# A decoder trunk on one core: biases loaded in nine pieces beside nine feed-forward tiles, and the residual's loads set between other loads

## The chip, the core and the metric

The kernel runs on one core of a Trainium2 chip. A core has five engines, each with its own queue of instructions that it works off in order: TensorE (PE in the rows; its weight loads are PEld), VectorE (DVE), ScalarE (ACT), GpSimd (POOL) and SyncE (SP), which here issues the transfers between DRAM and the on-chip memory (SBUF). The metric is the time of one execution on the device, in microseconds (us).

## The reference, cut to what matters

One step of a decoder trunk, for a prompt of 1024 tokens and 8 single new tokens, all float32, width 1024. Layer A is a gated linear recurrence, layer B an attention over a window of 128 tokens with 16 query heads on 4 shared key/value heads; each layer is followed by a SwiGLU feed-forward block, and every sub-layer is added to the residual:

```python
h = h + gate(c) * F(rmsnorm(h) * (1 + scale(c)) + shift(c))

def swiglu(x, w_in, w_out):                     # d_ff = 2816
    gate, up = jnp.split(x @ w_in, 2, axis=-1)
    return (jax.nn.silu(gate) * up) @ w_out

def rel_bias_for(dist, rel_bias):
    bias = rel_bias.astype(jnp.float32)[t5_bucket(dist)]
    ...
```

The attention adds that bias, one number for each head and distance, to its logits, and a learned sink for each head joins its softmax. The 8 new tokens attend to a cache of the last 128 rows of K and V, in which the new token's row takes the place of the oldest; the shifted caches are results too.

## The kernel before, in words

The tokens (1032 with the new ones) lie along the free axis, the features on the partitions, in 8 blocks of 128. A float32 product is three matmuls on rounded operands (`mm3`, L291 to L293): high by high, high by low, low by high. `weight()` (L178) makes the two halves of a weight tile: ScalarE casts it (L182), GpSimd subtracts the cast from it (L185). So a product needs, in this order, the weight's transfer, a cast on ScalarE and a subtraction on GpSimd.

The feed-forward block `ffn` (L1481) works through 22 tiles of 128 hidden columns. Tiles 2 to 21 go through `seven_products` (L1529): both halves of the SwiGLU input as one 2 by 2 block product with seven block products instead of eight (1, 2, 6, 7, 5, 3, 4 in the order used), each 24 matmuls of 128 x 258. The weights of these come from `seven` (L233): two raw tiles for a hidden tile, each in two transfers of 256 KB (L243), then three sums of them on VectorE (L253 to L255), a fourth later (L260), and seven units for the ring of 8 weight tiles. Units are prepared six ahead of their use. Of a tile's products, the first one's results are copied out by ScalarE (two COPYs, L1552), the others are added by VectorE (L1554 to L1571), with two Silu pairs on ScalarE (L1555, L1567), and the tile is stored to DRAM on SP (`ff`, L1572) as its last step.

`biases()` (L1296) prepares what layer B's attention needs beside the weights. It is called in the middle of the first feed-forward block, at tile 11: it loads a one-hot table, the bias table and a mask (L1302 to L1304), multiplies them in a small matmul with a sum (L1306, L1308), stores the result `rd` to DRAM, spreads it there to 128 rows (`gd`, 3 MB), loads the sinks (`sk`, `skd`) and the decode tokens' biases row by row for 8 tokens (L1319 to L1321), copies the two caches shifted by one row into the results (L1322, L1323), and negates the sinks (L1325).

The second place lies where layer B's attention ends and its output projection begins. `attention(1)` (second half of the heads) and `decode_attention()` run interleaved with the projection's products; the projection's results are added to the residual by VectorE (L845). The residual lies in DRAM (`hsc`) and is loaded in four chunks of 258 tokens by `reload_stack` (L1424, moves at L658, two transfers a chunk): the first chunk before, the others after `decode_attention` has issued the caches (L1769) and the new token's rows into them (`nd`, L1774).

The order of each engine's queue is fixed before the run by the Tile framework's scheduler, from its own estimates, and doesn't follow the order in which the code is written, except where `keep_in_program_order` (`fix` for a transfer) pins an instruction. A transfer on SP also waits for one of eight semaphores in turn, which the transfer eight issues earlier sets when it has landed.

Of the kernel before, what the change touches and what calls it, by code (L numbers as in the profile page):

```python
# [17 lines left out]
P = 128  # L18
# [8 lines left out]
NF = DFF // P  # L27
# [30 lines left out]
def bc(ap, axis, n):  # L58
    u = ap.unsqueeze(axis)
    shape = list(u.shape)  # L60
    shape[axis] = n
    return u.to_broadcast(shape)
# [3 lines left out]
def trunk_kernel(  # L66
# [40 lines left out]
    pe, act, dve, pool, sp = nc.tensor, nc.scalar, nc.vector, nc.gpsimd, nc.sync  # L107
# [10 lines left out]
    def nm(s):  # L118
        uid[0] += 1
        return f"{s}_{uid[0]}"  # L120

    def big(dt=F32, cols=TOK, parts=P):
        return p4.tile([parts, cols], dt, tag="c4", name=nm("c4"))
# [11 lines left out]
    def axp():  # L135
        return pp.tile([P, 512], F32, tag="ax", name=nm("ax"), bufs=4)
# [11 lines left out]
    class Stream:  # L148
# [15 lines left out]
        def next(self):  # L164
            n, room = self.used + 1, self.look
            while n < len(self.specs) and self.size[n] <= room:
                room -= self.size[n]
                n += 1
            self.ahead(n)
            u = self.done[self.used]  # L170
            self.used += 1
            return u
# [322 lines left out]
    fix = tc.keep_in_program_order  # L495
# [460 lines left out]
    X = Rows(KT)  # L956
# [339 lines left out]
    def biases():  # L1296

        stage = big(cols=1024)
        oneh = stage[:32, 0:384]
        relb = stage[:32, 384:400]  # L1300
        outs = stage[:16, 400:784]
        sp.dma_start(oneh, k_onehot)  # L1302
        sp.dma_start(relb, rel_bias)
        sp.dma_start(outs, k_outside)  # L1304
        ps = axp()
        pe.matmul(ps[:16, :384], relb, oneh, start=True, stop=True)  # L1306
        rrow = outs
        dve.scalar_tensor_tensor(rrow, ps[:16, :384], 8.0, outs, op0=ALU.mult, op1=ALU.add)  # L1308
        rd = dp.tile([16, 384], F32, name="rd")
        gd = dp.tile([16, P, 384], F32, name="gd")  # L1310
        sp.dma_start(rd, rrow)
        sp.dma_start(gd, bc(rd, 1, P))
        sk = cst.tile([P, 16], F32, name="sk")
        fix(sp.dma_start(sk, sinks_b[0].partition_broadcast(P)))
        skd = cst.tile([P, 1], F32, name="skd")
        late = cst.tile([P, 2 * P], F32, tag="early", name="late")
        biasd = late[:, 0:P]
        for b in range(NB):
            fix(sp.dma_start(skd[16 * b : 16 * b + 16, :], sinks_b[0].unsqueeze(1)))  # L1319
            sp.dma_start(biasd[16 * b : 16 * b + 16, 1:P], rd[:, P : 2 * P - 1])  # L1320
            sp.dma_start(biasd[16 * b : 16 * b + 16, 0:1], rd[:, 2 * P - 1 : 2 * P])  # L1321
        fix(sp.dma_start(ck_sample[:, 0 : WIN - 1], cache_swa_k[:, 1:WIN]))  # L1322
        fix(sp.dma_start(cv_sample[:, 0 : WIN - 1], cache_swa_v[:, 1:WIN]))  # L1323
        for t in (sk, skd):
            tc.keep_in_program_order(dve.tensor_scalar(t, t, -1.0, None, op0=ALU.mult))  # L1325
        return late, biasd, gd, sk, skd

    for hh in range(NH):
        first = hgrn_proj(hh) if hh else hgrn_first()
# [59 lines left out]
    def wo_second(o, gate, m, back, beside=iter(()), end=(3, 5)):  # L1389
        tdec = small([P, KT, NB], "tdec", 2)  # L1390
        us = [ws.next() for _ in range(4)]
        st = res[-1]
        N = StackNorm(st)
        x = Quads()

        def then(c):
            st.move(back, [c], False)
            yield from N.finish(c, *((3, 8) if c < G4.last else end))
            yield LAG
            yield from N.apply_steps(c, m, x)  # L1400

        for c in range(G4.n):
            for n in range(KT):
                wo_product(us[n // 2], o, c, n, gate, tdec, G4, anyp)
                N.square(c, n)
                step()
                if c and ((c - 1) * KT + n) % 2 == 0:
                    next(beside, None)
            if c == G4.last:
                residual_dec(tdec)  # L1410
                N.square_dec()
            queue(then(c))
        for _ in beside:
            pass
        return x, st
# [9 lines left out]
    def reload_stack(src, g):  # L1425

        st = Stack(g)
        res.append(st)
        st.move(src, [0], True)
        yield  # L1430
        st.move(src, range(1, g.n), True)


    def factors(x, st):
# [46 lines left out]
    def ffn(l, x, st, hs, norm, aside=None):  # L1481
# [115 lines left out]
                    pass  # L1597

        for j in range(PLAIN, NF):
            if j == NF // 2 and aside:  # L1600
                aside()
            seven_products(j, back if j == NF - 1 else None)

# [52 lines left out]
    back = [dp.tile([KT, P, T], F32, name=f"hs{i}") for i in range(2)]  # L1656
    X, st = wo_second(o, 16, 1, back[0], conditioning((6, 3), (2, 3)))
# [27 lines left out]
            yield from self.apply_steps(c, 2, self.x, keep=True)  # L1685

    bs = []
    nkv = ffn(0, X, st, back[0], ToKV, lambda: bs.extend(biases()))
    late, biasd, gd, nsk, nskd = bs


# [2 lines left out]
    X = Triples(KT)  # L1694
# [68 lines left out]
    def decode_attention():  # L1763
        kst, vst = [], []
        for dst, src in ((kst, cache_swa_k), (vst, cache_swa_v)):
            for hb in range(2):
                t = big(cols=T).rearrange("p (b f) -> p b f", b=4)
                bs = slice(4 * hb, 4 * hb + 4)
                sp.dma_start(t, src[bs].rearrange("b s h d -> s b (h d)"))  # L1769
                dst.append(t)  # L1770
        for dst, c0 in ((kst, 0), (vst, 256)):
            for hb in range(2):
                bs = slice(4 * hb, 4 * hb + 4)
                sp.dma_start(dst[hb][0:1], nd[bs, c0 : c0 + 256].unsqueeze(0))  # L1774
        ld = small([P, P], "s", 3)
        psl = axp()
        for hb in range(2):
            for a in range(2):
                ps = axp()
                for j in range(4):  # L1780
                    pe.transpose(
                        ps[:, j * P : (j + 1) * P], kst[hb][:, j, a * P : (a + 1) * P], ident
                    )
                kb = big(cols=512)
                act.copy(kb, ps)
                for j in range(4):
                    b = 4 * hb + j
                    c0 = 16 * b + 8 * a
                    pe.matmul(
                        psl[:, c0 : c0 + 8],  # L1790
                        kb[:, j * P : (j + 1) * P],
                        qdec[:, a, b].rearrange("p h g -> p (h g)"),
                        start=True,
                        stop=True,
                    )
                yield
        dve.tensor_copy(ld, psl[:, 0:P])
        ps = axp()
        pe.transpose(ps[:, 0:P], ld, ident)
        lt = small([P, P], "s", 3)  # L1800
        mx = small([P, 1], "dmx", 1)
        es = small([P, 1], "des", 1)
        den = small([P, 1], "dden", 1)
        dve.tensor_tensor_reduce(
            lt, ps[:, 0:P], biasd, -0.125, nskd, ALU.add, ALU.min, mx
        )
        act.activation(es, nskd, AF.Exp, scale=-1.0, bias=mx)
        act.activation(lt, lt, AF.Exp, scale=-1.0, bias=mx, accum_out=den)
        dve.tensor_tensor(den, den, es, op=ALU.add)
        dve.reciprocal(den, den)  # L1810
        dve.tensor_scalar(lt, lt, den, None, op0=ALU.mult)
        yield
        ps = axp()
        pe.transpose(ps[:, 0:P], lt, ident)
        dve.tensor_copy(ld, ps[:, 0:P])
        ps = axp()
        psv = ps[:, 0:64].rearrange("p (a b g) -> p a b g", a=2, b=NB)
        for b in range(NB):
            for a in range(2):
                for hf in range(2):  # L1820
                    kv = 2 * a + hf
                    pe.matmul(
                        psv[64 * hf : 64 * hf + 64, a, b, :],
                        vst[b // 4][:, b % 4, 64 * kv : 64 * kv + 64],
                        ld[:, 16 * b + 4 * kv : 16 * b + 4 * kv + 4],
                        start=True,
                        stop=True,
                    )
            if b % 2:
                yield  # L1830
        for a in range(2):
            dve.tensor_copy(adec[:, 4 * a : 4 * a + 4, :], psv[:, a].rearrange("p b g -> p g b"))
        yield
# [141 lines left out]
    loads = reload_stack(hsc, G4)  # L1975
    next(loads)
    next(second)
    dec = decode_attention()
    next(dec)
    for _ in loads:  # L1980
        pass

    def dec_first(o=o):
        for _ in dec:
            pass
        mixed_dec(o, adec, 0)
# [4 lines left out]
    X, st = wo_second(o, 64, 4, back[1], end=(5, 5))  # L1991
# [163 lines left out]
```

## Time and profile before

| | us |
|---|---|
| median of 3 runs | 2501.37 (2498.51 to 2503.21) |
| the profiled execution | 2500.0 |
| its span, first to last instruction | 2498.1 |
| TensorE busy in it | 2454.3 (98%) |
| VectorE busy | 1390.8 (56%) |
| ScalarE busy | 903.0 (36%) |
| GpSimd busy | 774.6 (31%) |

The mean granted clock of TensorE is 0.996 of the full one. A row of a timeline in the section below gives the start and the duration of an instruction or a run of like ones, the engine, its line in the kernel, what it writes and reads, the tile shapes and, in brackets, how long the engine had been idle before it and what it then waited for. Matmuls overlap in their pipeline, so the step from one start to the next is shorter than a matmul's duration. A name such as `wu` is a weight tile (high and low half), `raw` its unrounded tile, `mm` and `ax` two accumulation banks, `xq` the activations, `c` a buffer of general use and `hs` a chunk of the residual.

### The profile page before, as it was taken

The numbers are of one execution on the slowest core, as the hardware profiler recorded it, in microseconds if no ns is written. First come the engines' busy times: TensorE is split into PE (matmuls) and PEld (weight loads), VectorE is DVE, ScalarE is ACT, GpSimd is POOL, SyncE is SP. The second block draws the span as 40 slices with busy tenths as digits, with TensorE's granted clock in tenths as the row PEclk, the third lists the DMA queues.
The fourth block names the chain that finished last, engine by engine and source line by source line (L and its number), as shares of the span: only waits on it lengthen the run. The fifth ranks groups of instructions, "written<-read, shape, count | busy, mean of one in ns | idle before, by whom it ended". The sixth has DMA issues, their size and how long they took to land.

```text
span 2498.1 us, 52373 instructions
## 1 busy us (share of the span) xinstructions
PE 2454.3 (98%) x21557; PEld 2338.0 (94%) x21557; DVE 1390.8 (56%) x3177; ACT 903.0 (36%) x2012; POOL 774.6 (31%) x560
## 2 busy tenths in 40 slices
PE   7999999999999999999999999999999999999998
PEld 5999999998889999999999998878999999999998
DVE  6444444456486554656433735576885555565436
ACT  5333333332363332333211555454643333333112
POOL 1211111111225444544432131002364444445221
PEclk9999999999999999999999999999999999999999
DMA  9465522246833224326321322523222222264101
GB/s 332 146 214 178 170 76 72 70 131 211 267 106 94 82 84 144 97 83 233 123 77 51 93 56 65 165 85 110 69 86 77 77 77 81 82 228 148 65 26 69
DMA packets 314561, 293.43 MB, mean 117 GB/s; under 512 B 28681, under 2 KB 291738, under 8 KB 314290
## 3 DMA queue, kind: packets, MB, share of 16 engines
q1 hardware_dynamic: 313920, 289.86, 35.8%
q8 instruction: 170, 2.79, 0.5%
q14 instruction: 69, 0.57, 0.1%
q10 hardware_dynamic: 402, 0.22, 0.0%
HBM read 231.27 MB, written 63.99 MB: 118 GB/s over the span
## 4 chain that ended last, share of the span: by engine, by line
PE 89%; DVE 4%; DMA 3%; issue 2%; ACT 1%; SPq 0%; POOL 0%; ACTq 0%; DVEq 0%; POOLq 0%
PE mm L291 20%; PE mm L293 19%; PE mm L292 19%; PE ax L291 6%; PE ax L292 6%; PE ax L293 6%; PE ax L470 2%; PE ax L1943 1%; PE ax L1872 1%; PE ax L1098 1%; PE ax L1929 1%; PE ax L1225 1%; PE ax L1188 1%; DMA raw<-in_w_ffn_in_dram 1%; DMA gd<-rd 1%
## 5 line engine op out<-in xcount | busy, mean ns | idle before, releaser
L185 POOL TENSOR_TENSOR wu<-raw,wu 128x512 fp32r<-128x512 f32 x460 | 628.5, 1374 | 1380.1 <-ACT wu L182 1279.4
L291 PE MATMUL mm<-c,wu 128*128 128x344 f32 (+1 forms) x2104 | 673.8, 320 | 2.8 <-ACT c L917 1.7
L293 PE MATMUL mm<-c,wu 128*128 128x344 f32 (+1 forms) x2104 | 660.6, 314 | 1.9 <-issue 1.9
L292 PE MATMUL mm<-c,wu 128*128 128x344 f32 (+1 forms) x2104 | 662.0, 315 | 0.3 <-DVE c L920 0.3
L182 ACT CAST wu<-raw 128x512 fp32r<-128x512 f32 x464 | 286.0, 620 | 665.8 <-PE mm L293 358.5
L291 PEld LDWEIGHTS mm<-c,wu 128*128 128x128 f32 x2104 | 397.4, 189 | 16.1 <-issue 9.4
L292 PEld LDWEIGHTS mm<-c,wu 128*128 128x128 f32 x2104 | 397.8, 189 | 4.2 <-issue 2.6
L293 PEld LDWEIGHTS mm<-c,wu 128*128 128x128 f32 x2104 | 397.9, 189 | 1.8 <-issue 1.8
L291 PE MATMUL mm<-xq,wu 128*128 128x258 f32 x1376 | 390.3, 284 | 2.4 <-ACT wu L182 1.0
L293 PE MATMUL mm<-xq,wu 128*128 128x258 f32 x1376 | 389.6, 283 | 1.3 <-POOL wu L185 1.3
L292 PE MATMUL mm<-xq,wu 128*128 128x258 f32 x1376 | 388.2, 282 | 1.2 <-DVE xq L838 1.2
L291 PE MATMUL ax<-xq,wu 128*128 128x258 f32 x1120 | 316.4, 282 | 0.0
L293 PE MATMUL ax<-xq,wu 128*128 128x258 f32 x1120 | 315.8, 282 | 0.0
L292 PE MATMUL ax<-xq,wu 128*128 128x258 f32 x1120 | 315.6, 282 | 0.0
L291 PEld LDWEIGHTS mm<-xq,wu 128*128 128x128 f32 x1376 | 259.6, 189 | 4.1 <-DVE c L1502 1.2
L292 PEld LDWEIGHTS mm<-xq,wu 128*128 128x128 f32 x1376 | 260.7, 189 | 1.7 <-DVE xq L838 1.7
L293 PEld LDWEIGHTS mm<-xq,wu 128*128 128x128 f32 x1376 | 259.7, 189 | 2.8 <-POOL wu L185 1.5
L845 DVE SCALAR_TENSOR_TENSOR hs<-mm,ada,hs 128x344 f32<-128x344 f32 (+3 forms) x228 | 120.7, 533 | 173.3 <-PE mm L293 164.4
L292 PEld LDWEIGHTS ax<-xq,wu 128*128 128x128 f32 x1120 | 212.1, 189 | 0.0
L291 PEld LDWEIGHTS ax<-xq,wu 128*128 128x128 f32 x1120 | 211.5, 189 | 0.0
L293 PEld LDWEIGHTS ax<-xq,wu 128*128 128x128 f32 x1120 | 211.1, 188 | 0.0
L845 DVE SCALAR_TENSOR_TENSOR c<-mm,ada,c 128x344 f32<-128x344 f32 (+1 forms) x132 | 74.8, 571 | 112.1 <-PE mm L293 111.4
(329 smaller groups left out, 3603.1 us busy)
## 6 DMA issues: line engine op xcount, KB each, us to landing
c<-in_w_ada_dram SPq DMA_DIRECT2D x96, 512.0 KB
raw<-in_w_ffn_in_dram SPq DMA_DIRECT2D x160, 256.0 KB
ff<-c SPq DMA_DIRECT2D x44, 516.0 KB
c<-ff SPq DMA_DIRECT2D x44, 516.0 KB
raw<-in_w_ffn_out_dram SPq DMA_DIRECT2D x44, 512.0 KB
raw<-in_w_in_a_dram SPq DMA_DIRECT2D x32, 512.0 KB
hs<-hs SPq DMA_DIRECT2D x16, 516.0 KB
out_dram<-c SPq DMA_DIRECT2D x16, 512.0 KB
```

Of the source, the lines that this page charges most:

```text
L182: i = act.copy(u[:, 0, :], src)
L185: j = eng.tensor_tensor(u[:, 1, :], src, u[:, 0, :], op=ALU.subtract)
L291: put(pe.matmul(ps, wh, xh, start=first, stop=False))
L292: put(pe.matmul(ps, wh, xl, start=False, stop=False))
L293: put(pe.matmul(ps, wl, xh, start=False, stop=last))
L470: pe.matmul(ada_ps[q][32 * j : 32 * j + 32, 256 * i : 256 * i + 256], cT[:, k, :], u[i][:, j, :], start=(k == 0 and i == 0), stop=(k == KT ...
L845: dve.scalar_tensor_tensor(hc, ps[:, : g.pl[c]], ada[:, gate + n, 0:1], hc, op0=ALU.mult, op1=ALU.add)
L1098: pe.matmul(ps[32 * j : 32 * j + 32, c * 32 : (c + 1) * 32], KS[:, t0 : t0 + 32], QP[:, t0 : t0 + 32], start=True, stop=True, tile_positio ...
L1188: pe.matmul(ps[:, j * P : (j + 1) * P], kt[:, s], vt[:, s], start=True, stop=True)
L1225: pe.matmul(o, attT[:, c, :], vt[:, s], start=(c == 0), stop=True)
L1872: pe.matmul(psv[hf][:, gi, s0:256], q[2 * gp + gi][r, tb * P : (tb + 1) * P], kT[a][r, (tb - 1) * P + s0 : (tb + 1) * P], start=True, stop ...
L1929: pe.transpose(ps[:, g * P : (g + 1) * P], L[:, g, sb * P : (sb + 1) * P], ident)
```

## The change

`biases()` is a generator now. It is advanced once at each hidden tile from 11 on, before that tile's products, until it ends: nine pieces for tiles 11 to 19. Two more of its transfers are pinned to their place in the code. The residual's chunks are moved in three steps with a stop after each, and `decode_attention` stops between the caches and the new token's rows, so that its caller can put the loads in between: chunk 1 ahead of the caches, chunks 2 and 3 ahead of the rows. No operation on data is added or removed.

```diff
--- before.py
+++ after.py
@@ -1302,13 +1302,16 @@
         sp.dma_start(oneh, k_onehot)
         sp.dma_start(relb, rel_bias)
         sp.dma_start(outs, k_outside)
+        yield
         ps = axp()
         pe.matmul(ps[:16, :384], relb, oneh, start=True, stop=True)
         rrow = outs
         dve.scalar_tensor_tensor(rrow, ps[:16, :384], 8.0, outs, op0=ALU.mult, op1=ALU.add)
         rd = dp.tile([16, 384], F32, name="rd")
         gd = dp.tile([16, P, 384], F32, name="gd")
+        yield
         sp.dma_start(rd, rrow)
+        yield
         sp.dma_start(gd, bc(rd, 1, P))
         sk = cst.tile([P, 16], F32, name="sk")
         fix(sp.dma_start(sk, sinks_b[0].partition_broadcast(P)))
@@ -1317,13 +1320,16 @@
         biasd = late[:, 0:P]
         for b in range(NB):
             fix(sp.dma_start(skd[16 * b : 16 * b + 16, :], sinks_b[0].unsqueeze(1)))
-            sp.dma_start(biasd[16 * b : 16 * b + 16, 1:P], rd[:, P : 2 * P - 1])
-            sp.dma_start(biasd[16 * b : 16 * b + 16, 0:1], rd[:, 2 * P - 1 : 2 * P])
+            fix(sp.dma_start(biasd[16 * b : 16 * b + 16, 1:P], rd[:, P : 2 * P - 1]))
+            fix(sp.dma_start(biasd[16 * b : 16 * b + 16, 0:1], rd[:, 2 * P - 1 : 2 * P]))
+            if b % 2:
+                yield
         fix(sp.dma_start(ck_sample[:, 0 : WIN - 1], cache_swa_k[:, 1:WIN]))
         fix(sp.dma_start(cv_sample[:, 0 : WIN - 1], cache_swa_v[:, 1:WIN]))
         for t in (sk, skd):
             tc.keep_in_program_order(dve.tensor_scalar(t, t, -1.0, None, op0=ALU.mult))
-        return late, biasd, gd, sk, skd
+        yield
+        bs.extend((late, biasd, gd, sk, skd))
 
     for hh in range(NH):
         first = hgrn_proj(hh) if hh else hgrn_first()
@@ -1426,9 +1432,9 @@
 
         st = Stack(g)
         res.append(st)
-        st.move(src, [0], True)
-        yield
-        st.move(src, range(1, g.n), True)
+        for cs in ([0], [1], range(2, g.n)):
+            st.move(src, cs, True)
+            yield
 
 
     def factors(x, st):
@@ -1597,7 +1603,7 @@
                     pass
 
         for j in range(PLAIN, NF):
-            if j == NF // 2 and aside:
+            if j >= NF // 2 and aside:
                 aside()
             seven_products(j, back if j == NF - 1 else None)
 
@@ -1685,7 +1691,8 @@
             yield from self.apply_steps(c, 2, self.x, keep=True)
 
     bs = []
-    nkv = ffn(0, X, st, back[0], ToKV, lambda: bs.extend(biases()))
+    bias_steps = biases()
+    nkv = ffn(0, X, st, back[0], ToKV, lambda: next(bias_steps, None))
     late, biasd, gd, nsk, nskd = bs
 
 
@@ -1768,6 +1775,7 @@
                 bs = slice(4 * hb, 4 * hb + 4)
                 sp.dma_start(t, src[bs].rearrange("b s h d -> s b (h d)"))
                 dst.append(t)
+        yield
         for dst, c0 in ((kst, 0), (vst, 256)):
             for hb in range(2):
                 bs = slice(4 * hb, 4 * hb + 4)
@@ -1975,10 +1983,12 @@
     loads = reload_stack(hsc, G4)
     next(loads)
     next(second)
+    next(loads)
     dec = decode_attention()
     next(dec)
     for _ in loads:
         pass
+    next(dec)
 
     def dec_first(o=o):
         for _ in dec:
```

The order of the engines' queues moves with it in three places. The first is ScalarE's queue, from tile 13's casts to those of tile 14 in the first feed-forward block. In a row stand the line, the operation, what it writes and reads; c4_1316, c4_1342 and c4_1368 are the buffers that the COPYs of tiles 12, 13 and 14 fill, raw_1320/1321 (and s3_1323) are tile 13's weights and raw_1346/1347 tile 14's. Before:

```order
L182 CAST wu_1322_11784<-raw_1320_11778 128x512
L1552 COPY c4_1316_11746<-mm_1318_11750 128x258
L1552 COPY c4_1316_11746<-ax_1319_11751 128x258
L1555 ACTIVATE c4_1315_11745<-c4_1315_11745 128x258 x2
L1567 ACTIVATE c4_1316_11746<-c4_1316_11746 128x258 x2
L1552 COPY c4_1342_11987<-mm_1344_11991 128x258
L1552 COPY c4_1342_11987<-ax_1345_11992 128x258
L182 CAST wu_1326_11821<-raw_1321_11781 128x512
L182 CAST wu_1329_11852<-raw_1320_11778 128x512
L182 CAST wu_1332_11883<-s3_1323_11787 128x512
```

The second cast of tile 13 (wu_1326) stands here behind tile 13's own COPYs. In the changed kernel it stands a tile earlier, right behind tile 12's:

```order
L182 CAST wu_1322_11750<-raw_1320_11744 128x512
L1558 COPY c4_1316_11712<-mm_1318_11716 128x258
L1558 COPY c4_1316_11712<-ax_1319_11717 128x258
L182 CAST wu_1326_11787<-raw_1321_11747 128x512
L1561 ACTIVATE c4_1315_11711<-c4_1315_11711 128x258
```

and the casts of tile 14 from the second on (wu_1352) stand behind tile 14's own COPYs, where before wu_1352 stood a tile earlier:

```order
L182 CAST wu_1348_11992<-raw_1346_11986 128x512
L1558 COPY c4_1342_11954<-mm_1344_11958 128x258
L1558 COPY c4_1342_11954<-ax_1345_11959 128x258
L1561 ACTIVATE c4_1341_11953<-c4_1341_11953 128x258 x2
L1573 ACTIVATE c4_1342_11954<-c4_1342_11954 128x258 x2
L1558 COPY c4_1368_12206<-mm_1370_12210 128x258
L1558 COPY c4_1368_12206<-ax_1371_12211 128x258
L182 CAST wu_1352_12029<-raw_1347_11989 128x512
L182 CAST wu_1355_12060<-raw_1346_11986 128x512
```

So the same arrangement has moved by one tile. The second place is ScalarE's queue again, at tile 20 (its COPYs fill c4_1524, tile 19's c4_1498; raw_1502/1503 are tile 20's weights). Before:

```order
L182 CAST wu_1504_13471<-raw_1502_13465 128x512
L1552 COPY c4_1498_13433<-mm_1500_13437 128x258
L1552 COPY c4_1498_13433<-ax_1501_13438 128x258
L182 CAST wu_1508_13508<-raw_1503_13468 128x512
L1555 ACTIVATE c4_1497_13432<-c4_1497_13432 128x258
```

and now:

```order
L182 CAST wu_1504_13471<-raw_1502_13465 128x512
L1558 COPY c4_1498_13433<-mm_1500_13437 128x258
L1558 COPY c4_1498_13433<-ax_1501_13438 128x258
L1561 ACTIVATE c4_1497_13432<-c4_1497_13432 128x258 x2
L1573 ACTIVATE c4_1498_13433<-c4_1498_13433 128x258 x2
L1558 COPY c4_1524_13674<-mm_1526_13678 128x258
L1558 COPY c4_1524_13674<-ax_1527_13679 128x258
L182 CAST wu_1508_13508<-raw_1503_13468 128x512
```

Here the cast wu_1508 has gone from behind tile 19's COPYs to behind tile 20's own. The third place is SP's queue at the end of layer B's attention, from the biases of the window (`gd`) on. Before:

```order
L1845 DMA c4_2217_18566<-gd_11469 128x4x256
L1769 DMA c4_2218_18568<-in_cache_swa_k_dram 128x4x256
L1769 DMA c4_2219_18570<-in_cache_swa_k_dram 128x4x256
L1769 DMA c4_2220_18572<-in_cache_swa_v_dram 128x4x256
L1769 DMA c4_2221_18574<-in_cache_swa_v_dram 128x4x256
L1774 DMA c4_2218_18568<-nd_17045 1x4x256
L1774 DMA c4_2219_18570<-nd_17045 1x4x256
L1774 DMA c4_2220_18572<-nd_17045 1x4x256
L1774 DMA c4_2221_18574<-nd_17045 1x4x256
L658 DMA hs_2226_18593<-hsc_8732 128x4x258
L658 DMA hs_2227_18595<-hsc_8732 128x4x258
L658 DMA hs_2228_18597<-hsc_8732 128x4x258
```

and now:

```order
L1853 DMA c4_2217_18566<-gd_11710 128x4x256
L658 DMA hs_2218_18568<-hsc_8732 128x4x258
L658 DMA hs_2219_18570<-hsc_8732 128x4x258
L1776 DMA c4_2220_18572<-in_cache_swa_k_dram 128x4x256
L1776 DMA c4_2221_18574<-in_cache_swa_k_dram 128x4x256
L1776 DMA c4_2222_18576<-in_cache_swa_v_dram 128x4x256
L1776 DMA c4_2223_18578<-in_cache_swa_v_dram 128x4x256
L658 DMA hs_2224_18580<-hsc_8732 128x4x258
L658 DMA hs_2225_18582<-hsc_8732 128x4x258
L658 DMA hs_2226_18584<-hsc_8732 128x4x250
L658 DMA hs_2227_18586<-hsc_8732 128x4x250
L1782 DMA c4_2220_18572<-nd_17045 1x4x256
```

The residual's chunk 1 has passed the caches, chunks 2 and 3 have passed the new token's rows. In TensorE's queue, 141 matmuls of 258 columns stood between the projection's first product and the first transpose of the decode tokens' keys (L1781 before, L1789 now); 220 stand there now.

## Rows read from the trace of the kernel before

**Rows 1.** The page, its first line

```profile
span 2498.1 us, 52373 instructions
```

**Rows 2.** Windows of the feed-forward block: stretch, its length, PE, PEld, DVE, ACT, POOL, clock, DMA

```profile
820.00:850.00 30.00, 30.00 (x252) 30.00 (x251) 16.40 (x35) 9.01 (x18) 12.97 (x11) 1.00 0.17 54
...
980.00:990.00 10.00, 9.78 (x81) 9.78 (x82) 4.74 (x7) 3.76 (x8) 8.73 (x8) 1.00 0.27 78
```

**Rows 3.** Timeline of TensorE, tile 13: start, duration, instruction, idle before, releaser

```profile
977.15 0.28 PE L293 MATMUL ax<-xq,wu 128*128 128x258 f32 x1
978.41 0.39 PE L291 MATMUL mm<-xq,wu 128*128 128x258 f32 x1 [0.98 <-ACT wu L182]
...
980.22 0.39 PE L293 MATMUL mm<-xq,wu 128*128 128x258 f32 x1 [1.31 <-POOL wu L185]
980.44 0.28 PE L291 MATMUL mm<-xq,wu 128*128 128x258 f32 x1
```

**Rows 4.** Chain of waits, tiles 11 to 13: start, duration, what

```profile
939.44 13.01 DMA gd<-rd
...
963.01 13.75 DMA raw<-in_w_ffn_in_dram
...
978.43 1.75 POOL wu L185
```

**Rows 5.** Timeline of ScalarE, tile 13

```profile
977.46 0.38 ACT L1552 COPY c<-ax 128x258 f32<-128x258 f32 x1 [1.05 <-PE ax L293]
977.73 0.62 ACT L182 CAST wu<-raw 128x512 fp32r<-128x512 f32 x1
```

**Rows 6.** Timeline of GpSimd, tile 12

```profile
952.29 1.29 POOL L185 TENSOR_TENSOR wu<-raw,wu 128x512 fp32r<-128x512 f32 x1 [1.64 <-ACT wu L182]
```

**Rows 7.** Timeline of VectorE, end of layer B's attention

```profile
1620.77 0.49 DVE L845 SCALAR_TENSOR_TENSOR hs<-mm,ada,hs 128x258 f32<-128x258 f32 x1 [0.94 <-PE mm L293]
1629.34 1.67 DVE L845 SCALAR_TENSOR_TENSOR hs<-mm,ada,hs 128x258 f32<-128x258 f32 x4 [8.09 <-DMA hs<-hsc]
...
1633.11 0.34 DVE L1883 CUSTOM_DVE_ANT_0 c<-ax,c,sk 128x128 f32<-128x128 f32 x1
```

**Rows 8.** Timeline of SP's queue, the same stretch

```profile
1611.87 2.45 SPq L1769 DMA_DIRECT2D c<-in_cache_swa_k_dram  x2
...
1620.64 4.54 SPq L1774 DMA_DIRECT2D c<-nd  x4
1625.23 4.09 SPq L658 DMA_DIRECT2D hs<-hsc  x6
```

**Rows 9.** Timeline of TensorE, the same stretch

```profile
1627.23 1.06 PE L1789 MATMUL ax<-late,c 128*128 128x8 f32 x8 [0.31 <-ACT c L1785]
1628.22 0.72 PE L1872 MATMUL ax<-c,c 64*128 64x128 f32 x8
...
1629.88 0.42 PE L291 MATMUL mm<-c,wu 128*128 128x258 f32 x1 [0.36 <-DVE hs L845]
...
1633.53 0.29 PE L293 MATMUL mm<-c,wu 128*128 128x258 f32 x1
```

**Rows 10.** Windows of the same stretch

```profile
1625.00:1630.00 5.00, 4.33 (x38) 3.74 (x37) 0.66 (x2) 1.02 (x2) 0.00 (x0) 1.00 0.76 207
1630.00:1635.00 5.00, 5.00 (x31) 5.00 (x31) 2.99 (x13) 1.66 (x9) 0.00 (x0) 0.66 1.10 348
```

**Rows 11.** Timeline of VectorE, tile 13

```profile
975.06 0.43 DVE L1571 TENSOR_TENSOR c<-c,c 128x258 f32<-128x258 f32 x1
...
978.35 0.69 DVE L255 TENSOR_TENSOR raw<-raw 128x512 f32<-128x512 f32 x1
```

**Rows 12.** Timeline of TensorE, two of the attention's scores

```profile
1653.53 0.70 PE L1872 MATMUL ax<-c,c 64*128 64x256 f32 x4
...
1699.10 1.13 PE L1872 MATMUL ax<-c,c 64*128 64x256 f32 x8
```

**Rows 13.** A window of the attention

```profile
1680.00:1685.00 5.00, 5.00 (x42) 3.24 (x39) 4.82 (x24) 3.34 (x13) 0.00 (x0) 1.00 0.40 129
```

## The prediction

> **What bounds the kernel now.** I read the span and the busy table of the page first, then windows over the two stretches that the change touches (the first feed-forward block, the end of layer B's attention), then each engine's timeline there, and the chain of waits last. TensorE is busy for nearly all of the span [rows 1]: a quiet stretch of feed-forward holds 252 matmuls in 30 us, 0.119 us from one to the next (0.12 below), at a granted clock of 1.00 [rows 2]. So only what opens a hole in TensorE's row, or lowers its clock, moves the end; a transfer or a VectorE operation that is merely earlier does not. The profiled execution took 2500.0 us for a span of 2498.1, so 1.9 us lie outside the span and stay; it is 1.4 us under the median of the runs shown, 2501.37. I sum changes against 2500.0 and add them to the median.
>
> In the stretches that the change touches I find two places with holes.
>
> *Tile 13 of the first feed-forward block.* The last matmul of product 1 starts at 977.15, the first of product 2 at 978.41, the third at 980.22, the fourth at 980.44 [rows 3]. Four steps that should take 4 x 0.12 took 3.29 us: 2.81 us lost. The releasers printed there are ScalarE's cast and GpSimd's subtraction. It looks as if the weight load were to blame, since its 13.75 us in the chain end at 976.76, behind the 13.01 us of gd [rows 4]. But the cast of these weights starts at 977.73, straight behind a COPY at 977.46 that itself waited 1.05 us for the last matmul of product 1 [rows 5]; and in ScalarE's order before, that cast stands behind the two COPYs of its own tile. An in-order queue cannot give it earlier, however early the weights are there. From the COPY the chain is cast 0.62, then GpSimd 1.75 where a like one took 1.29 [rows 4, 6], then TensorE. The lateness of the load and the place in the order are both there, and either alone would open most of the hole.
>
> *Residual of the decode stretch.* VectorE adds layer B's first output tiles to the residual; after the operation at 1620.77 it stands still for 8.09 us, waiting for hs, until 1629.34 [rows 7]. Those loads leave SP at 1625.23, behind the caches (from 1611.87) and the new token's rows (1620.64) [rows 8]. TensorE has room for most of that; what reaches it is 0.31 us at 1627.23 and 0.36 us at 1629.88, together 0.67. Then, from 1629.88 to 1633.53, 17 steps take 3.65 us, 0.215 each instead of 0.12: 17 x 0.095 = 1.6 [rows 9]. The granted clock of that stretch is 0.66, of the one before it 1.00 [rows 10]. Lost: 2.3 us.
>
> **The change part by part: the biases.** The number of transfers, of matmuls and of VectorE operations stays. The burst that stands in the chain from gd to the weight load is spread over nine tiles, and SP's queue holds at most a few small ones ahead of a tile's weights, so the load for tile 13 no longer lies behind 3 MB of gd. ScalarE's order changes with it. At tile 13 the cast now stands right behind tile 12's COPYs: 2.81 us go. But the same pattern appears at tile 14, and again at tile 20, where before the cast stood one tile earlier. At each of the two, product 2 cannot start until its weights are cast, and the cast cannot start until the last matmul of product 1 has gone through the COPY. The price is bounded by tile 13's row from above, 2.81. From below: COPY and cast give the same 1.26 us step, and GpSimd's operation takes at least its 1.29 instead of 1.75, so 2.81 - 0.46 = 2.35. Which end depends on VectorE: at tile 13 its two sums for the weights (0.69 each, the second at 978.35) ran beside GpSimd's 978.43 [rows 4, 11]. In the new order they stand behind the last operation of the tile before, which ended 1.9 us ahead of that tile's COPY (975.06 + 0.43 against 977.46 [rows 5, 11]), and with weights present nothing holds them; they need 2 x 0.69 = 1.4 us and are done before GpSimd begins. I take 2.35. Net: 2 x 2.35 - 2.81 = +1.9 us, at most 2 x 2.81 - 2.81 = +2.8; nothing below +1.9 unless a hole is shorter than its own chain.
>
> GpSimd's 1.75 against 1.29 is where the Trainium skill bears on a term ("SBUF — State Buffer", section "Who interferes with whom"): a VectorE operation with two SBUF inputs and a GpSimd operation that reads SBUF exclude each other, and the later one waits whole. The rows agree in kind: 0.46 more where the sum of 978.35 overlaps. By that rule the sum is the 2.35 taken if the VectorE sums are through first, and 2.81 if not.
>
> Work hidden at no cost: nd, gd, sk and cache copies have no reader before layer B, and SP issues each at a tile whose weights are a tile ahead; if that cover fails, a tile's weights come late by what stands in front of them, with 13.01 us of gd [rows 4] as the largest piece. The store of the tile's result, which stands behind these on SP, has its reader after the block. The little matmul of the biases moves one tile and costs the same.
>
> **The residual's loads and the caches.** On SP chunk 1 takes the caches' place, its issue at about 1611.9 in place of 1625.23; the first cache load issued at that time had landed when SP passed its successor at 1620.64 [rows 8], so chunk 1 is there by 1620.6 to 1622. VectorE wants it about 0.94 us after the operation that ended at 1621.26 [rows 7]. The 8.09 us of standing still go, and with them the 0.67. The caches, chunks 2 and 3 and the new token's rows follow, each about 1 to 4 us later than in the old row; the first readers of the new rows are the decode transposes. In TensorE's order 220 matmuls now stand ahead of these instead of 141: they come 79 x 0.12 = 9.5 us later, less the 0.67 and what the clock drop takes, so nearly 9 us of cover for rows that I expect to land some 5 us later. If that is wrong, TensorE waits by the difference.
>
> The same 79 matmuls are then missing later: from the first score at 1628.22 [rows 9] (then about 1636.6, 9.5 us later less some 1.1 for the holes that lie ahead of it) to the sixth there are 33 instead of 69, and from the fourteenth to the last 6 instead of 41; the rest lie between. Their sum is no change. So the gain is the 2.3 us of holes and slow steps, if the drop of the clock goes with its pause. VectorE also has its six residual operations before the attention's first reductions and not among them, 6 x 0.45 = 2.7 us (0.49 for one and 1.67 for four in [rows 7], between which 0.45 lies). After score 6, at 1653.53 [rows 12], VectorE sets the pace, busy 4.82 of 5 us [rows 13], so some of that may come back. From -2.3 to -2.3 - 2.7 = -5.0; I take a quarter, -3.0. On the other side: the attention starts 8.4 us later, and where VectorE sets the pace, a later start cannot be made good by fewer matmuls. VectorE's first reduction, at 1633.11 before [rows 7], would come about 3.8 later, less 2.7, so +1.1; a clock drop of 1.7 at the new place in addition: +2.8. The nearest row is the pause itself, so I stay near -3.0.
>
> **Sum.** +1.9 - 3.0 = -1.1: 2498.9 us for a profiled execution, and 2500.3 against the median. A difference that can be told from no change here is 0.2%, 5.0 us.
>
> **Rivals.** *A: the feed-forward block loses no time at all*, the casts not binding: -2.81 - 3.0 = -5.8, 2495.6. For it: the load of tile 13 really was late by the chain. Against: ScalarE's new order at tiles 14 and 20, where TensorE must wait through COPY and cast. 0.09.
>
> *B: the late attention.* Place: from score 1 to score 16. VectorE sets the pace, so the later start is not won back: +1.9 + 2.8 = +4.7, 2506.1. For it: 4.82 of 5 us [rows 13]. Against: between the first and sixth score TensorE sets the pace, and 36 x 0.12 = 4.3 us leave it there. It decides from the point at which the time from first to last score shrinks by less than the 8.4 us by which the first score is late. 0.14.
>
> *C: the clock.* Each new hole is followed by a stretch at the lower of the two levels, as after 1629.88: 1.6 us each, so +3.2 on top of -1.1: +2.1, 2503.5. For it: the 0.66 of [rows 10]. Against: in the stretch after tile 13's hole the clock reads 1.00 [rows 2], with a hole of the same size. The Trainium skill ("TensorE: Matmul & The Clock Gate", "Part 1: The HAM clock gate") has the clock halved by idleness of the array; [rows 2, 10] show both outcomes. 0.12.
>
> *D: nothing moves*: holes come and go, within 0.5 us of the old time, 2501.4. 0.10.
>
> **How the numbers follow.** Forecast 0.55, A 0.09, B 0.14, C 0.12, D 0.10. Forecast's own range: -5.0 + 1.9 = -3.1 to +2.8 - 2.3 = +0.5, so 2498.3 to 2501.9. Only A reaches past -5.0, and only B's upper part past +5.0: faster 0.10, within 0.2% 0.82, slower 0.08. The range from 2497.0 to 2504.5 leaves out A and most of B, and keeps the median's own spread of 2498.5 to 2503.2.
>
> **What would show it.** Tile 13 without a hole; at tiles 14 and 20 a step of about 1.26 us behind product 1 and then one of 1.3 to 1.8, released by ScalarE and GpSimd; no 8 us wait of VectorE for hs; scores starting near 1636 and the last of them, at 1699.10 before [rows 12], about 3 us earlier when both traces are set to zero at the start of layer B's attention. Wrong would be: no hole at tile 14 or 20 (A); the last score no earlier (B); a clock under 1.00 after a hole (C); a TensorE wait for the new token's rows.

## The result

| | before | changed | changed against before |
|---|---|---|---|
| median of 14 runs, us | 2499.64 | 2505.40 | +5.76 |
| range, us | 2498.12 to 2503.21 | 2500.97 to 2508.32 | |
| ratio, 95% interval | | | 1.0021, 1.0014 to 1.0028 |

The change makes the kernel slower, by 0.2%. The forecast was 2500.3 us and a range that ended at 2504.5, so the time lies outside it. As a change, -1.1 was forecast and +5.8 measured; the forecast's base, the median of three runs (2501.37), lay 1.7 us above that of the 14. Of the two terms of the sum, the feed-forward one came out nearly as worked out; the other, the end of layer B's attention, has the wrong sign. Two executions below, one with the biases alone (2646.32 us, mean granted clock 0.85) and one of the last kernel (2951.12 us, 0.75), are left out of the medians.

### The profile page after: what moved, and what is told of

Its sections match the earlier page's. It is cut to its first block, busy times and chain, and to the rows that moved or that the text cites. A ratio compares the mean times of both kernels' runs of the same rounds, so it can differ in the third digit from the quotient of the medians.

```text
span 2503.0 us, 52365 instructions
## 1 busy us (share of the span) xinstructions
PE 2457.8 (98%) x21557; PEld 2340.0 (93%) x21557; DVE 1390.2 (56%) x3177; ACT 901.4 (36%) x2012; POOL 777.6 (31%) x560
```

## The profile after, beside the one before

In both kernels TensorE works through the same sequence of 15,360 matmuls on weight tiles; only what stands between them differs. So I compare the start of the matmul with the same number in two traces: where the difference grows, time is lost. A first look at the page alone would mislead:

```profile
span 2503.0 us, 52365 instructions
```

The span is 4.9 us longer than [rows 1], but the differences say where:

```
weight-tile matmul no.      before    after   difference
 4800 (feed-forward, A)     912.92   915.67   +2.75
 5520 (behind tile 14)     1003.13  1005.41   +2.28
 6720 (behind tile 20)     1147.24  1151.88   +4.64
 9360 (before attention B) 1620.57  1625.37   +4.80
10080 (behind it)          1777.33  1782.58   +5.25
15120 (near the end)       2438.40  2443.21   +4.81
```

The first 2.75 us arise ahead of the biases, where the order of every engine is the same in both kernels; in ten more profiles, of kernels with that same order there, the difference at this place lies between -0.7 and +3.2. That is spread between executions, and no part of the change. What belongs to the change in this profile is -0.47 + 2.36 in the block and +0.45 at the attention.

*Tiles 13, 14 and 20.* Tile 13's hole of [rows 3] is gone: the same two products follow each other without a stop.

```profile
979.89 0.28 PE L293 MATMUL ax<-xq,wu 128*128 128x258 f32 x1
980.01 0.28 PE L291 MATMUL mm<-xq,wu 128*128 128x258 f32 x1
```

At tile 14, TensorE's timeline of the changed kernel (columns as in [rows 3]) has the step of 1.26 us and one of 1.13:

```profile
1000.07 0.28 PE L293 MATMUL ax<-xq,wu 128*128 128x258 f32 x1
1001.33 0.39 PE L291 MATMUL mm<-xq,wu 128*128 128x258 f32 x1 [0.98 <-ACT wu L182]
1001.55 0.28 PE L292 MATMUL mm<-xq,wu 128*128 128x258 f32 x1
1002.68 0.39 PE L293 MATMUL mm<-xq,wu 128*128 128x258 f32 x1 [0.84 <-POOL wu L185]
1002.90 0.28 PE L291 MATMUL mm<-xq,wu 128*128 128x258 f32 x1
```

From 1000.07 to 1002.90 are 2.83 us for four steps: 2.35 lost. Tile 20 has the same two steps (1123.47 to 1124.73, 1124.95 to 1126.08). ScalarE's timeline, and SP's for the load that the cast needs:

```profile
1000.38 0.38 ACT L1558 COPY c<-ax 128x258 f32<-128x258 f32 x1 [1.05 <-PE ax L293]
1000.65 1.14 ACT L182 CAST wu<-raw 128x512 fp32r<-128x512 f32 x2
```
```profile
978.83 1.34 SPq L243 DMA_DIRECT2D raw<-in_w_ffn_in_dram  x2
```

The last weights were issued at about 980, 20 us before the cast, and VectorE's sums of them (next rows) start at 998.33 without a wait. So what is late is the cast's place in the queue, which ScalarE's two rows show: COPY, then CAST. VectorE's and GpSimd's timelines give the lower end of the price, as chosen:

```profile
998.33 0.68 DVE L254 TENSOR_TENSOR raw<-raw,raw 128x512 f32<-128x512 f32 x1
999.12 0.69 DVE L255 TENSOR_TENSOR raw<-raw 128x512 f32<-128x512 f32 x1
```
```profile
1001.35 2.53 POOL L185 TENSOR_TENSOR wu<-raw,wu 128x512 fp32r<-128x512 f32 x2 [21.82 <-ACT wu L182]
```

VectorE's sums end at 999.81, so GpSimd's two operations take 2.53 together, where [rows 4] shows 1.75 for one. This agrees with the rule from the Trainium skill that the prediction weighed ("SBUF — State Buffer", "Who interferes with whom"): no VectorE operation with two SBUF inputs in the way, no wait.

*The attention.* SP's queue and VectorE's timeline, against [rows 7, 8]:

```profile
1616.48 2.99 SPq L658 DMA_DIRECT2D hs<-hsc  x2
1619.52 3.67 SPq L1776 DMA_DIRECT2D c<-in_cache_swa_k_dram  x2
1623.28 2.83 SPq L1776 DMA_DIRECT2D c<-in_cache_swa_v_dram  x2
1626.21 6.03 SPq L658 DMA_DIRECT2D hs<-hsc  x4
1632.29 2.53 SPq L1782 DMA_DIRECT2D c<-nd  x4
```
```profile
1639.95 0.48 DVE L845 SCALAR_TENSOR_TENSOR hs<-mm,ada,hs 128x258 f32<-128x258 f32 x1 [0.96 <-PE mm L293]
1643.25 0.35 DVE L1891 CUSTOM_DVE_ANT_0 c<-ax,c,sk 128x128 f32<-128x128 f32 x1 [2.81 <-PE ax L1880]
```

Less the 4.8 us by which this trace is later, chunk 1 is issued at 1611.7, as worked out, and VectorE never waits for hs again. But TensorE's timeline has the first score at 1642.50 (1637.7 on the old scale, not 1636.6) and the last at 1705.87:

```profile
1642.50 0.71 PE L1880 MATMUL ax<-c,c 64*128 64x128 f32 x8
...
1649.11 1.52 PE L1880 MATMUL ax<-c,c 64*128 64x256 f32 x4
1650.56 0.58 PE L293 MATMUL mm<-c,wu 128*128 128x258 f32 x1
1650.94 0.42 PE L291 MATMUL mm<-c,wu 128*128 128x258 f32 x1
1651.15 0.42 PE L292 MATMUL mm<-c,wu 128*128 128x258 f32 x1
...
1705.87 1.13 PE L1880 MATMUL ax<-c,c 64*128 64x256 f32 x4
```

From 1650.56 on, steps are 0.21 us again: the drop of the clock that stood at 1629.88 [rows 9] has not gone with VectorE's pause but has come again 21 us later. Windows of the same trace:

```profile
1640.00:1645.00 5.00, 5.00 (x44) 4.44 (x42) 2.05 (x11) 1.95 (x7) 0.00 (x0) 1.00 0.06 20
1645.00:1650.00 5.00, 5.00 (x32) 4.13 (x32) 3.32 (x20) 3.99 (x20) 0.00 (x0) 0.97 0.01 2
1650.00:1655.00 5.00, 5.00 (x25) 3.97 (x24) 2.06 (x11) 1.93 (x7) 0.00 (x0) 0.69 0.00 0
```

TensorE counts as busy for 5.00 of 5 us in all three, and DMA rests: nobody waits for a load. With 1.2 GHz being half of the full rate, a mean clock of m over 5 us means (1 - m) x 2 x 5 us at the lower level: here (0.03 + 0.31) x 10 = 3.4 us, as much as before (0.34 x 10 [rows 10]).

## The experiments

Theory 1, formed from that: the block costs +1.9 by the two new holes less the old one, and the moved loads cost because TensorE's order leaves too few projection matmuls in the attention. Rivals: the order of the transfers, and lateness of the weights.

**Each part alone.** *Biases only*: the kernel before, with the generator and nothing of the loads. Of its edit, the line that spreads the pieces:

```diff
-            if j == NF // 2 and aside:
+            if j >= NF // 2 and aside:
```

> Only the biases in nine pieces; the residual's loads stand as in the kernel before. Theory 1 (the holes of tiles 14 and 20 are all that this part costs): +1.9 us on the kernel before (-2.8 at tile 13, +2.35 at each of tiles 14 and 20), granted clock unchanged. Rival (each hole is followed by slow steps in most executions, or the transfers cost somewhere else): +4 to +5.5, nearly all of the measured +5.4 to +5.8.

Measured: 2503.78 us against 2500.30, 1.0016 (1.0007 to 1.0025). *Loads only*: the kernel before, with the three steps of `reload_stack` and the stop in `decode_attention`.

> Only the residual's loads moved; the biases stand as one burst as in the kernel before. Theory 1: +3 to +4 us, the rest of the measured +5.4 to +5.8, of which the one profile of the changed kernel shows only +0.5, because the attention with few projection matmuls between its steps falls to the lower clock for longer in most executions. Rival (this part costs the +0.5 of that profile and no more): 0 to +1.

Measured: 2502.02, 1.0009 (1.0000 to 1.0018). The two add up to 5.2 us, nearly the whole. For the biases the middle, +3.5, lies between the theory's +1.9, just inside the interval, and the rival's +4 to +5.5; for the loads the middle, +1.7, lies between the two as well. In the trace of the run with the biases alone the hole at tile 14 costs the 2.35, the one at tile 20 3.86, because slow steps follow it (1120 to 1130 at a clock of 0.83, so 3.4 us at the lower level).

**The casts pinned.** In the changed kernel, and in the kernel before:

```diff
-        if len(ws.done) <= 4:
+        if len(ws.done) <= 4 or pinned[0]:
             tc.keep_in_program_order(i)
...
-                act.copy(u, ps)
+                i = act.copy(u, ps)
+                if pinned[0]:
+                    tc.keep_in_program_order(i)
...
+            pinned[0] = l == 0 and NF // 2 <= j < NF - 1
```

> The changed kernel, with ScalarE's casts of the weights and its COPYs of tiles 11 to 20 pinned in the order of the code, so that no tile's cast stands behind its own COPYs. Theory 1: no hole at tiles 13, 14 and 20, so 4.7 us less than the changed kernel, about +1 on the kernel before. Rival (the weights come late in any order, the order of the casts is not what binds): the holes stay, within 1 us of the changed kernel.

Measured: 2505.47, 1.0020 (1.0012 to 1.0029): the total follows the rival, the mechanism does not. In its trace no hole is left at tiles 13, 14 and 20; at matmul 6480 it is 2.8 us ahead of where it stood at 4800, against before. Then 4.6 us go at once where the block's output product begins. TensorE's and VectorE's timelines there:

```profile
1160.13 0.43 PE L292 MATMUL mm<-c,wu 128*128 128x344 f32 x1 [1.71 <-DVE c L1579]
...
1162.51 0.43 PE L292 MATMUL mm<-c,wu 128*128 128x344 f32 x1 [1.15 <-DVE hs L846]
```
```profile
1152.78 1.24 DVE L1595 TENSOR_TENSOR c<-c,c 128x1032 fp32r<-128x1032 f32 x1 [7.01 <-ACT c L1594]
```

VectorE stands for 7.01 us before the operation on the first reloaded `ff` tile (3.02 us in the changed kernel), and works off its backlog after that. It waits for ScalarE's cast of that tile, and ScalarE's timeline shows the cast waiting for the transfer:

```profile
1151.69 1.05 ACT L1594 CAST c<-c 128x1032 fp32r<-128x1032 f32 x1 [6.46 <-DMA c<-ff]
```

At the block's end TensorE is 8.2 us earlier than in the changed kernel (matmul 6720), this cast only 4.2 (1155.89 there). The pins changed SP's order too; how much of the lateness that makes is not shown. So this kernel took away the holes and gave the time back; its total says nothing of the holes because of that, and because 17 us at the lower clock in the attention (below) came on top.

> The kernel before, with the same pins as in the pinned changed kernel. Theory 1: at tile 13 the cast can start when its weights are there, at 976.76 instead of 977.73, so about 1 us of the 2.8 goes and 1.6 to 1.9 stay (late weights: the burst's own price); -1 on the kernel before. Rival (only ScalarE's order makes the hole): it goes whole, -2.8.

Measured: 2498.56, 0.9988 (0.9980 to 0.9997), faster than before. TensorE's and ScalarE's timelines at tile 13:

```profile
979.42 0.28 PE L293 MATMUL mm<-xq,wu 128*128 128x258 f32 x1
980.91 0.39 PE L294 MATMUL mm<-xq,wu 128*128 128x258 f32 x1 [1.21 <-POOL wu L186]
981.13 0.29 PE L292 MATMUL mm<-xq,wu 128*128 128x258 f32 x1
```
```profile
978.35 0.62 ACT L183 CAST wu<-raw 128x512 fp32r<-128x512 f32 x1 [3.70 <-DMA raw<-in_w_ffn_in_dram]
```

The step behind the cast is gone, the one behind GpSimd stands: 1.47 of 2.81 us stay, near the 1.6 to 1.9 expected. Now the cast waits for the weights and for nothing else. So the late weights alone cost 1.47, the cast's order alone 2.35 (tile 14); before, the two overlapped in one hole. The total is no measure of the pins alone: in this profile the block gains 1.1 us, and 1.8 come from the attention, where the clock happened not to drop.

**The loads' order against TensorE's order.** Three more orders of the loads, biases as before; TensorE's order follows from them through the scheduler and falls into two kinds. The edit of the run with chunk 1 alone, against the moved loads, is shown below; the run with the caches first leaves out the `next(loads)` ahead of the caches instead, the third one puts it between the two steps of `dec`:

```diff
     next(loads)
     dec = decode_attention()
     next(dec)
+    next(dec)
     for _ in loads:
         pass
-    next(dec)
```

> Biases as before; of the loads only chunk 1 stands ahead of the caches, chunks 2 and 3 behind the new token's rows as before. In TensorE's order 168 projection matmuls stand ahead of the first decode transposes (141 before, 220 with the whole change) and 47 more between the first and the second transposes. Theory (few projection matmuls in the attention's first 20 us let the clock fall): the granted clock stays at 1.00 there or falls for at most 3.4 us, the attention takes 1 to 2.5 us less than before: 2498 to 2500. Rival (the order of the transfers decides: chunk 1 ahead of the caches makes caches and rows late): as with the whole of the moved loads, +1 to +2 on before.

> Biases as before; loads in the order caches, chunks 1 to 3, new token's rows, so the caches are as early as before. TensorE's order is nearly that of the whole change (219 matmuls ahead, 4 between). Theory: clock below 1.00 for 3.4 us or more in the attention's start, 0.5 to 6 us more than before in that stage. Rival (order of the transfers): the caches come as before, no fall of the clock, not slower than before.

> Biases as before; loads in the order caches, chunk 1, new token's rows, chunks 2 and 3. TensorE's order is nearly that of the run with chunk 1 alone (166 ahead, 47 between). Theory: like that run, clock 1.00 or one fall of at most 3.4 us, 1 to 2.5 us less than before. Rival (order of the transfers): like the run with the caches first.

Measured: chunk 1 alone 2499.42, 0.9994 (0.9986 to 1.0003); caches first 2503.62, 1.0019 (1.0011 to 1.0028); chunk 1 between 2499.58, 0.9998 (0.9989 to 1.0007). The first and the third can't be told from the kernel before, the second is slower. The windows of the run with chunk 1, and of the one with the caches first:

```profile
1640.00:1645.00 5.00, 5.00 (x44) 4.72 (x44) 3.34 (x20) 2.77 (x12) 0.00 (x0) 1.00 0.52 123
1645.00:1650.00 5.00, 5.00 (x38) 4.05 (x37) 4.15 (x22) 3.61 (x16) 0.00 (x0) 1.00 0.01 2
1650.00:1655.00 5.00, 5.00 (x33) 3.12 (x32) 3.60 (x19) 3.48 (x14) 0.00 (x0) 1.00 0.00 0
```
```profile
1645.00:1650.00 5.00, 5.00 (x22) 4.08 (x21) 2.74 (x16) 2.92 (x13) 0.00 (x0) 0.68 0.01 2
1650.00:1655.00 5.00, 5.00 (x23) 3.88 (x22) 2.06 (x11) 1.70 (x6) 0.00 (x0) 0.64 0.00 0
```

As far as the caches and chunk 1 go, the transfers' order is told apart from TensorE's: caches first or not, both kinds occur, and the time goes with TensorE's order. Chunks 2 and 3 ahead of the new token's rows is what the slower ones share, and there no run moves the transfers without TensorE's order. But in the six profiles of the slower kind no wait of an engine between 1630 and 1712 is put down to a transfer of the rows, the caches or the residual, so late transfers are not what costs there.

**The changed kernel again**, two more profiles, 2507.74 and 2506.36 us:

> The changed kernel unaltered, one more profile. Theory (TensorE's order decides, the extent of the fall varies by execution): holes at tiles 14 and 20 again, 1.26 and 1.13 us in their two steps; the clock below 1.00 in the attention's start again, for 3.4 us at the lower level or a multiple. Rival (one profile was a chance event): 1.00 there, stage shorter than before.

> The changed kernel unaltered, a second further profile; the same expectations as for the first.

The holes of 1.26 and 1.13 (1.12) stand at both tiles in both. After one of them each time, tile 14 in the first and tile 20 in the second, slow steps follow (another 1.5 us). Windows of the first one in the attention:

```profile
1645.00:1650.00 5.00, 5.00 (x25) 3.86 (x26) 2.54 (x17) 3.53 (x18) 0.00 (x0) 0.72 0.01 2
1650.00:1655.00 5.00, 5.00 (x18) 4.14 (x19) 2.84 (x15) 0.66 (x4) 0.00 (x0) 0.50 0.00 0
1655.00:1660.00 5.00, 5.00 (x27) 3.75 (x26) 0.98 (x4) 2.25 (x8) 0.00 (x0) 0.75 0.00 0
```

All profiles of that stage together. "Inside" counts projection matmuls between the first and the last score; the third column is the time at the lower level between 1600 and 1730, from windows as above; the last is the change of the difference to the profile before, from matmul 9360 to 10080:

```
kernel                 inside   us at 1.2 GHz   us lost
before                   120        3.4           0
before, pinned           120        0            -1.8
biases only              120        0            -0.4
changed, 3 profiles       49    3.4 6.9 10.3     +0.5 +2.0 +3.6
loads only                49        3.4          +0.4
changed, pinned           49       17.1          +6.3
caches first              43        6.8          +2.9
chunk 1                  101        0            -2.6
chunk 1, pinned          101        0            -2.5
chunk 1 between           99        3.4          +0.5
small pieces (last run)  101        0            -2.6
```

With the biases alone VectorE's pause stays, and in that profile it reaches TensorE as a hole of 1.37 us (0.36 before [rows 9]). Yet the clock does not drop; TensorE's timeline and a window there:

```profile
1635.19 0.39 PE L291 MATMUL mm<-c,wu 128*128 128x258 f32 x1 [1.37 <-DVE hs L845]
```
```profile
1635.00:1640.00 5.00, 4.81 (x43) 4.67 (x43) 3.29 (x14) 1.65 (x8) 0.00 (x0) 1.00 1.10 350
```

So the drop does not go with the pause from either side: here a longer pause without a drop, in the changed kernel a drop without the pause. The longer hole is also why this profile gains only 0.4 us there and the pinned kernel before 1.8, both at the full clock.

**A version that beats both.** First chunk 1 with the pins of before:

> The run with chunk 1 alone, and ScalarE's casts and COPYs pinned as in the pinned kernel before. Theory: both gains add up, -1.7 from the pins (1.4 of it at tile 13) and -1 to -2.5 from chunk 1: 2496 to 2498, below both kernels. Rival: as the pinned kernel before alone, 2498.5.

Measured: 2498.37, 0.9992 (0.9983 to 1.0001): not clear of before. Then the biases in smaller pieces from tile 2 on, with pins for tiles 6 to 17 only, and the loads of the run with chunk 1:

```diff
+        for b in range(NB):
+            fix(sp.dma_start(ck_sample[b, 0 : WIN - 1], cache_swa_k[b, 1:WIN]))
+            fix(sp.dma_start(cv_sample[b, 0 : WIN - 1], cache_swa_v[b, 1:WIN]))
+            if b % 2:
+                yield
...
+            sp.dma_start(gd[2 * b : 2 * b + 2], bc(rd[2 * b : 2 * b + 2], 1, P))
...
+            pinned[0] = l == 0 and 6 <= j < 18
```

> Biases in smaller pieces from tile 2 on (the cache copies by batches of two in tiles 2 to 5, gd in eight parts of two heads), casts and COPYs of tiles 6 to 17 pinned, loads as in the run with chunk 1 alone. Theory: no hole in the block (-2.8 on before) and no fall of the clock at the attention (-2 to -2.5): 2494.5 to 2497. Rival (the end of the block takes it back, as in the pinned changed kernel): 2498 to 2500.

Measured: 2496.28 against 2499.78, 0.9987 (0.9978 to 0.9995). Windows of the block at the place of tile 13, and of the attention:

```profile
970.00:980.00 10.00, 10.00 (x86) 10.00 (x85) 6.09 (x12) 2.96 (x6) 2.21 (x2) 1.00 0.24 74
980.00:990.00 10.00, 10.00 (x85) 10.00 (x84) 6.39 (x10) 2.89 (x8) 7.54 (x6) 1.00 0.41 127
1645.00:1650.00 5.00, 5.00 (x33) 3.23 (x32) 3.89 (x20) 3.47 (x15) 0.00 (x0) 1.00 0.00 0
```

No hole (86 and 85 matmuls in 10 us, where [rows 2] has 81), nothing given back at the block's end, and -2.6 us at the attention without a drop of the clock.

## Why the prediction was wrong, step by step

- *The holes at tiles 14 and 20* came from the order alone, at 2.35 each, and tile 13's went: right, with the lower end of the bounds as chosen. The mean over the changed kernel's three profiles from matmul 4800 to 6960 is 2.8 us instead of 1.9 (1.9, 3.3, 3.4). The difference is rival C, in part: of the 13 holes with a cast behind its own COPY, in nine profiles, 4 were followed by slow steps, for 1.5 us each (estimated 1.6).
- *Tile 13's price of 2.81* was this one execution's. In four other profiles with the burst and without pins the hole lost 2.4 to 2.6 us, so the change removes somewhat less than the sum said.
- *The term of -3.0 for the loads* failed. Its step was: "So the gain is the 2.3 us of holes and slow steps, if the drop of the clock goes with its pause." It does not. The pause went and the drop came 21 us later, in the stretch that now has few large matmuls; the +0.5, +2.0 and +3.6 of three profiles (mean +2.0) stand where -3.0 was forecast. That is 5.0 of the 6.9 us between the change forecast and the one measured; the block gives 0.9 more, and the last 1.0 these profiles do not place. The time itself was missed by 5.1 us only because the base was 1.7 too high. The prediction had also priced a later attention with a drop at the new place, at +2.8, and set it aside because "The nearest row is the pause itself".
- *"Their sum is no change"*, said of the 79 matmuls moved ahead of the attention, was the oversight: the forecast counted them as work and left out what the attention is without them between its steps. By matmul counts the stage should be 71 x 0.12 = 8.5 us shorter from first to last score (70.88 us before); it is 7.5, 4.4 and 5.9 shorter.
- *Rival B* (0.14) had the place, the sign and its deciding point, under 8.4 us. Its change was +4.7, the measured one +5.8; its 2506.1 us stand on the same high base. Its reason was half right: VectorE's first reduction is later, 5.3 us on the old scale (1643.25 against 1633.11) and not 3.8 or 1.1, but what costs is mostly the clock, by an estimate. In the six profiles with 43 or 49 matmuls inside, from 3.4 us at the lower level to 17.1 the loss goes from 0.45 to 6.3: 0.43 us for each. By that line they would stand at -1.0 without a drop, between the -0.4 and -1.8 of the old order without one; no profile of them shows it.
- *A, D* and the cover of the new token's rows: A is excluded by the rows at tiles 14 and 20, D by the time. No wait of TensorE for the rows appears; 9 us of cover held.

Open: which property of the stretch the clock follows. All six profiles with 43 or 49 matmuls inside drop, two of seven with 99 to 120 do (the best version's among the seven). That is a clear association with TensorE's order and none with waiting for transfers, and not a proof that the drop makes the loss; a kernel with nothing but filler matmuls added there was not tried. Also open is what decides, for one and the same order of TensorE, between 3.4 and 17.1 us at the lower clock.

## What to carry to other kernels

When matmuls move out of a stretch of small dependent work, do not book them as neutral: ask what is left between that work's steps, and look at the granted clock, not only at busy shares. In a statically ordered program, an edit of transfers is an edit of every queue; compare each engine's order, and price an instruction that stands behind a consumer of its own stage as a hole, whatever the loads do. Compare several profiles per kernel before a term of 3 us is read from one: here 2.75 us of difference lay ahead of the first changed instruction.

## What the runs showed of the hardware that was not expected

A drop to the lower clock with TensorE booked as busy for 5.00 of 5 us: at 1650 to 1655 the clock is 0.50 in two profiles of the changed kernel and one of the pinned one, with 18 to 20 instructions in the window and no wait printed. And a hole of 1.37 us without a drop (the biases alone), beside 0.36 us with one (before): the booked idle time did not tell where the clock would fall. The Trainium skill has a case of this kind ("TensorE: Matmul & The Clock Gate", "A second HAM failure mode: psum-queue depth-cycling"): short pauses of the array between groups of matmuls, at which the clock swings. The windows here agree in that the clock goes down and up again within a stretch of matmuls; pauses of the array they do not show, and whether accumulation banks are the reason here no run shows. The same order of instructions spent 3.4, 6.9 and 10.3 us at the lower clock in three executions, so one execution does not give the price of such a stretch.
